# Reading transposed activations once from PSUM, a searched order of tasks at the edges, and adaLN units one place earlier, in a four-layer diffusion backbone

## The chip, the cores and the metric

The kernel runs on one core of a Trainium2 chip. Times are device microseconds (us) of that core from start to end of one execution. Lower is better. The kernel computes in fp32 accuracy: every large product is made of three fp32r products of high and low parts, so TensorE (PE) has three matmuls for each tile of a weight.

## What is computed

Four layers, each a token mixer (pooling, latent attention MLA, neighbourhood attention NA, pooling again) and a SwiGLU FFN, on 256 latent tokens and 256 context tokens of width 1024. Around each of the eight sub-layers stand two RMS norms, and shift, scale and gate come from a condition through one large matrix per layer (adaLN):

```python
def reference(x, c, ctx, c_ctx, ada_w, ada_b, norm_g, ...):
    for i in range(DEPTH):
        sh_m, sc_m, g_m, sh_f, sc_f, g_f = adaln(c[:, None, :], ada_w[i], ada_b[i])
        h_lat = modulate(rmsnorm(x, norm_g[i, 0]), sh_m, sc_m)      # h * (1 + scale) + shift
        ...                                                           # the same for ctx
        y_lat, y_ctx = mixer[i % 3](h_lat, h_ctx)
        x = x + g_m * rmsnorm(y_lat, norm_g[i, 1])
        f_lat = swiglu(modulate(rmsnorm(x, norm_g[i, 2]), sh_f, sc_f), ffn_w_gu[i], ffn_w_down[i])
        x = x + g_f * rmsnorm(f_lat, norm_g[i, 3])
        ...
    return x
```

The context stream ends after the mixer of layer 2 (counted from 0): from layer 2's FFN on only the latent tokens are worked on.

## The kernel before

**Tiling.** Tokens are four tiles of 128: tiles 0 and 1 are the latent stream (c = 0), 2 and 3 the context stream (c = 1). Activations that enter a product lie transposed, as eight blocks d of 128 features, each with a high and a low part (`R[d]`, `R[8 + d]`, tile `rh`). The hidden width of the FFN is 22 blocks of 128. While both streams run, a product has 512 columns; with one stream 256.

**Weights.** All weights and the adaLN matrices come in chunks of 512 KB through one DMA queue, issued by SP, into a ring of five tiles `raw`, in an order that a dry run of the program has recorded. ACT makes the high part of a chunk (L161, `wh`), DVE the low part (L165, `wl`), into five buffers each, up to five chunks ahead (`pump`). A slot of the ring is free when the last reader of its tile is issued, and the next load is issued then (`loads`).

**adaLN units.** A unit (l, u) is one sixth of a layer's adaLN matrix, in the order u = 1, 0, 2, 4, 3, 5, of eight steps with one `raw` tile each. A step is done either on PE from the raw tile (L406, `adp<-raw,sc`) or on DVE, which adds into `ff_a` (L424, L426), one instruction a step or, up to unit (2, 0), one for each stream; a unit with steps on DVE ends with pick products on PE (L406, `adp<-ff_a,pick`). Units that are not gates then go through an ACT copy (L451) and two PE transposes (L454). In an FFN each new weight chunk earns `RATE` steps (1.27, 1.27, 0.83, 0.5 by layer), done on DVE; `finish` ends a unit that has begun on DVE ahead of the last segment of the down projection; `need` does on PE, at once, what is missing when a result is wanted. The down projection has two segments of hidden blocks (12 and 10) with two streams and one of 22 with one stream; its products are L362 to L364 (`acc<-wh,rx`, `acc<-wl,rx`).

**Edges.** Between the last down (or output) products of one sub-layer and the first products of the next, the work on PE, DVE and ACT is ordered by a planner. `Edge` lists tasks (one or a few instructions) with an engine, a duration, dependences and a priority; `Sched.run` places them one after the other on modelled engines, by priority, and emits them by their modelled start. The tasks of an edge are: the last products of the projection (`second`); `chain`, for each token tile: squares (L864), output times gate (L870, L872), residual add (L881), squares for the next norm (L804), normalised x into `big` (L811 on DVE or L813 on ACT); `make_h`, for each pair of blocks d: transposes on PE into one PSUM bank (L916, `aux`), and from there the modulated high and low parts; and the first four chunks of the next sub-layer's products (`head`, L1087, L1088, L1090), with the weight splits they need. At the last pool mixer the products with the band and pool matrices (`mix_u`, `mix_y`, L1029) stand between a `make_h` and a second `chain` and `make_h`.

In `make_h` a transposed half bank of 256 columns (one d) is read from PSUM twice: once on ACT with scale, bias and rounding to fp32r (`high`, L930), and once on ACT (L935) or DVE (L937) into one of three tiles `t` (`whole`); DVE then subtracts the two (`low`, L940). Only at the first edge, where the shift arrives late, another form reads it once, into a tile `y` (`late_h`: L951 or L953, then L956 and L959).

Of the kernel before, what the change touches and what calls it, by code (L numbers as in the profile page):

```python
# [12 lines left out]
ALU = mybir.AluOpType  # L13
# [37 lines left out]

AHEAD = {'mwo': ('aux', 'aux'), 'nwo': ('aux', 'aux')}
# [21 lines left out]
class Net:  # L74
    def __init__(self, nc, pools, ins, out, uses=None, order=None):
# [17 lines left out]
        self.order = order  # L93
        self.rec = []
# [110 lines left out]
    def w(self, name, i, n=1):  # L205
# [411 lines left out]
class Slot:  # L617


    def __init__(self, before, old):  # L620
        self.before, self.old = before, old
        self.first, self.users, self.tile = None, [], None


class Sched:
# [9 lines left out]
    def add(self, eng, fn, deps=(), prio=5, order=(), ready=0.0, new=None, slots=(), between=False):  # L635
# [7 lines left out]
        t.new, t.between = new, between  # L643
        self.tasks.append(t)
        return t

    def slot(self, tag, bufs):
        a = self.tags.setdefault(tag, [])
        a.append(Slot(a[-1] if a else None, a[-bufs] if len(a) >= bufs else None))
        return a[-1]  # L650

    def run(self):
# [6 lines left out]
        busy = {e: [] for e in "PDAS"}  # L659
        left = list(enumerate(self.tasks))  # L660

        def place(e, at, dur, between):

            for a, b in busy[e]:
                if between:
                    at = b if a <= at < b - 0.1 else at
                    continue
                if at + dur - self.OVER[e] <= a:
                    break
                at = max(at, b)  # L670
            return at

        while left:
            can = [(t.prio, i, t) for i, t in left if all(d.end is not None for d in t.deps) and all(o.start is not None for o in t.order)]
            assert can, [(t.eng, t.prio) for _, t in left][:5]
            _, i, t = min(can, key=lambda x: x[:2])
            at = max([t.ready] + [o.start for o in t.order])
            options = []
            for e, dur in t.eng.items():
                s = place(e, max([at] + [d.end + (self.HOP if d.on != e else 0) for d in t.deps]), dur, t.between)  # L680
                options.append((s + dur, s, e))
            t.end, t.start, t.on = min(options)
            busy[t.on].append((t.start, t.end))
            busy[t.on].sort()
            left = [x for x in left if x[0] != i]

        for t in sorted(self.tasks, key=lambda t: (t.start, t.end)):
            self.emit(t)

# [9 lines left out]
class Edge:  # L699
# [6 lines left out]
    def __init__(self, n, l, u, tiles):  # L706
# [12 lines left out]
        self.spread = []  # L719

# [53 lines left out]
    def pooled(self, j):  # L774
        n = self.n
        return not n.dry and n.prepped + j - self.have < len(n.uses) and n.uses[n.prepped + j - self.have][0][1].startswith("pool")
# [54 lines left out]
    def chain_of(self, c, close):  # L831
# [3 lines left out]
        for t in (2 * c, 2 * c + 1):  # L835
            prio = 1 + t // 2 * 1.5
            gready = 0.0 if loads else 3.5
            done, sqs = {}, []
            for h in range(2):
                ps, made, slot, *ends = self.parts[t, h]  # L840
                y, hs = n.Y[2 * t + h], slice(512 * h, 512 * h + 512)
                p, gdeps = (1 + 0.4 * c, loads[c][h:h + 1]) if loads else (prio, [])
                if self.fold:
# [11 lines left out]
                    done[h] = s.add({"D": 0.56}, gy, [f, q] + gdeps, p, ready=gready)  # L855
# [3 lines left out]
                for e, (sl, g) in enumerate(gs):  # L859
# [5 lines left out]
                    sqs.append(s.add({"A": 0.68 if g is None else 0.5}, sq, made, p, slots=(slot,)))  # L865
# [7 lines left out]
                    ys.append(s.add({"D": 0.69 if g is None else 0.42}, gy, made + gdeps, p, slots=(slot,), ready=gready))  # L873
                done[h] = ys[-1]
# [3 lines left out]
            for h in range(2):  # L878
# [5 lines left out]
                new[h] = s.add({"D": 0.7}, up, [fac, done[h]], prio)  # L884
# [3 lines left out]
    def make_h(self, l, i):  # L888
# [8 lines left out]
        for c in self.streams:  # L897
# [5 lines left out]
            for dp in range(4):  # L903
                tag = "acc" if late and i == 0 and c == 0 else "aux"
# [14 lines left out]
                for e in range(2):  # L919
# [4 lines left out]
                    if late:  # L924
# [1034 lines left out]
```

## Time and profile before

| what | value |
|---|---|
| time, median of 3 runs | 1735.46 us (1735.09 to 1737.63) |
| the profiled execution: its time | 1739.13 us |
| the profiled execution: span of its trace | 1737.4 us |
| PE busy | 1635.4 us, 94% of the span |
| DVE, ACT busy | 1065.8 us (61%), 754.7 us (43%) |
| granted TensorE clock, mean | 0.97 of full speed |
| bytes moved by DMA | 286.66 MB, mean 165 GB/s |

In the trace an instruction is named by its line, its engine and output<-inputs; `[1.46 <-DMA raw]` behind a line is idle time of the engine ahead of it, and what ended it. PE is busy nearly everywhere; time can be lost or won where it is not, and where its clock is below full speed.

### The profile page before, as it was taken

How to read it: one execution, taken by the hardware profiler on the slowest of the kernel's cores; microseconds unless marked ns; L12 is line 12 of the kernel's file. 1: busy time of each engine (PE TensorE's matmuls, PEld its weight loads, DVE VectorE, ACT ScalarE, POOL GpSimd, SP SyncE). 2: the span in 40 equal slices, each digit the busy share in tenths (PEclk: the TensorE clock that was granted, in tenths of full speed). 3: DMA queues.
4: the chain of work that ended last, by engine and by line, in shares of the span. 5: the costliest groups of instructions: out<-in, count | busy, mean ns of one | idle time of the engine just before them, and what ended most of it. 6: DMA issues, size and time to landing. Idle time of an engine off the chain costs nothing.

```text
span 1737.4 us, 24716 instructions
## 1 busy us (share of the span) xinstructions
PE 1635.4 (94%) x9686; PEld 1378.5 (79%) x9686; DVE 1065.8 (61%) x1715; ACT 754.7 (43%) x1348; POOL 34.1 (2%) x42
## 2 busy tenths in 40 slices
PE   5899999999989999899999999999979999769998
PEld 2588888888886777888888888888769997659996
DVE  3567766664657674677545536765657773567554
ACT  4663223222554445522232226654565543464442
POOL 0000000000000110000000000000000000000000
PEclk8999999999999999999999999999989999879999
DMA  8926566554221131365654541433338896228662
GB/s 327 338 68 222 191 194 188 165 171 162 73 85 43 55 122 61 110 205 184 199 193 159 195 157 65 137 113 118 101 127 287 285 303 208 108 95 311 195 186 93
DMA packets 82525, 286.66 MB, mean 165 GB/s; under 512 B 9788, under 2 KB 12648, under 8 KB 82408
## 3 DMA queue, kind: packets, MB, share of 16 engines
q1 hardware_dynamic: 79208, 278.71, 48.2%
q0 software_dynamic: 1760, 5.29, 1.0%
q8 instruction: 76, 1.25, 0.3%
q10 hardware_dynamic: 1440, 1.09, 0.2%
q14 instruction: 41, 0.34, 0.1%
HBM read 283.95 MB, written 1.09 MB: 164 GB/s over the span
## 4 chain that ended last, share of the span: by engine, by line
PE 86%; DVE 6%; ACT 6%; DMA 1%; issue 1%; DVEq 0%; SPq 0%; ACTq 0%
PE acc L354 14%; PE acc L355 14%; PE acc L356 13%; PE acc L362 8%; PE acc L363 8%; PE acc L364 8%; PE adp L406 3%; PE acc L1088 2%; PE acc L1087 2%; PE acc L1090 2%; PE aux L354 1%; PE aux L355 1%; PE aux L356 1%; PE aux L916 1%; DVE wl L165 1%
## 5 line engine op out<-in xcount | busy, mean ns | idle before, releaser
L165 DVE TENSOR_TENSOR wl<-raw,wh 128x1024 fp32r<-128x1024 f32 x321 | 389.1, 1222 | 218.2 <-ACT wh L161 216.7
L161 ACT ACTIVATE wh<-raw 128x1024 fp32r<-128x1024 f32 x321 | 334.3, 1053 | 334.9 <-PE acc L364 159.0
L354 PE MATMUL acc<-rh,wh 128*128 128x512 f32 (+1 forms) x1296 | 439.0, 339 | 0.0
L355 PE MATMUL acc<-rh,wh 128*128 128x512 f32 (+1 forms) x1296 | 436.6, 337 | 0.0
L356 PE MATMUL acc<-rh,wl 128*128 128x512 f32 (+1 forms) x1296 | 436.5, 337 | 0.0
L354 PEld LDWEIGHTS acc<-rh,wh 128*128 128x128 f32 x1296 | 246.0, 190 | 30.5 <-issue 4.1
L356 PEld LDWEIGHTS acc<-rh,wl 128*128 128x128 f32 x1296 | 246.0, 190 | 25.8
L355 PEld LDWEIGHTS acc<-rh,wh 128*128 128x128 f32 x1296 | 246.1, 190 | 25.0
L426 DVE SCALAR_TENSOR_TENSOR ff_a<-raw,sc,ff_a 128x1024 f32<-128x1024 f32 x168 | 209.5, 1280 | 0.2
L362 PE MATMUL acc<-wh,rx 128*128 128x512 f32 x528 | 207.0, 392 | 0.0
L363 PE MATMUL acc<-wl,rx 128*128 128x512 f32 x528 | 205.9, 390 | 0.0
L364 PE MATMUL acc<-wh,rx 128*128 128x512 f32 x528 | 205.7, 390 | 0.0
L391 ACT ACTIVATE rx<-big 128x256 fp32r<-128x256 f32 (+1 forms) x82 | 42.4, 517 | 251.9 <-DVE big L556 251.9
L556 DVE TENSOR_TENSOR big<-big,acc 128x256 f32<-128x256 f32 (+1 forms) x90 | 48.9, 543 | 116.8 <-PE acc L356 96.1
L364 PEld LDWEIGHTS acc<-wh,rx 128*128 128x128 f32 x528 | 99.4, 188 | 20.8
L362 PEld LDWEIGHTS acc<-wh,rx 128*128 128x128 f32 x528 | 99.4, 188 | 20.2
L363 PEld LDWEIGHTS acc<-wl,rx 128*128 128x128 f32 x528 | 99.4, 188 | 20.2
L1087 PE MATMUL acc<-rh,wh 128*128 128x256 f32 x304 | 82.8, 299 | 6.4 <-ACT wh L161 3.2
L1088 PE MATMUL acc<-rh,wl 128*128 128x256 f32 x304 | 81.7, 296 | 6.2 <-DVE wl L165 5.9
L916 PE MATMUL aux<-ident,big 128*128 128x128 f32 x192 | 37.3, 329 | 46.1 <-DVE big L811 27.0
L377 DVE TENSOR_TENSOR rx<-big,rx 128x256 fp32r<-128x256 f32 (+1 forms) x82 | 45.0, 549 | 47.8 <-ACT rx L391 47.8
L916 PEld LDWEIGHTS aux<-ident,big 128*128 128x128 f32 x192 | 25.7, 166 | 58.2 <-DVE big L811 28.7
(239 smaller groups left out, 2267.4 us busy)
## 6 DMA issues: line engine op xcount, KB each, us to landing
raw<-in_ada_w SPq DMA_DIRECT2D x192, 512.0 KB, 4.8
raw<-in_gu SPq DMA_DIRECT2D x176, 512.0 KB, 4.6
raw<-in_dn SPq DMA_DIRECT2D x88, 512.0 KB, 4.3
raw<-in_nwin SPq DMA_DIRECT2D x24, 512.0 KB, 3.7
G<-gate POOLq DMA_DIRECT2D x10, 512.0 KB, 4.8
raw<-in_mwo SPq DMA_DIRECT2D x8, 512.0 KB, 3.5
raw<-in_nwo SPq DMA_DIRECT2D x8, 512.0 KB, 3.9
raw<-in_mwin SPq DMA_DIRECT2D x6, 512.0 KB, 3.4
```

The source lines that it names most:

```text
L161: nc.scalar.activation(out=hi[:, 0:n, :], in_=raw, func=AF.Copy)
L165: nc.vector.tensor_tensor(out=lo[:, 0:n, :], in0=raw, in1=hi[:, 0:n, :].bitcast(F32), op=ALU.subtract)
L354: nc.tensor.matmul(out, wh, ah, start=start, stop=False)
L355: nc.tensor.matmul(out, wh, al, start=False, stop=False)
L356: nc.tensor.matmul(out, wl, ah, start=False, stop=stop)
L362: nc.tensor.matmul(out, ah, wh, start=start, stop=False)
L363: nc.tensor.matmul(out, ah, wl, start=False, stop=False)
L364: nc.tensor.matmul(out, al, wh, start=False, stop=stop)
L426: nc.vector.scalar_tensor_tensor(out=acc[:, i, :], in0=v, scalar=c, in1=acc[:, i, :], op0=ALU.mult, op1=ALU.add)
L916: nc.tensor.transpose(slot.tile[:, o:o + 128], xs.tile[:, j:j + 128], n.ident)
L1087: nc.tensor.matmul(o, wh, hi, start=(k == 0), stop=False)
L1088: nc.tensor.matmul(o, wl, hi, start=False, stop=False)
```

## The change

Three things are changed.

1. `make_h` uses one form at every edge (`split_h`): x times the norm factor is read once from PSUM, by ACT or DVE, with scale and shift, into a tile Y in SBUF; `high` is made from it on ACT or DVE, `low` on DVE. The tiles `t` are gone. With one stream the third pair of banks is taken from `adp`.
2. The planner tries 1500 random changes of the priorities (with a fixed seed) and keeps those that its model finds better; the model has a new rule, that ACT and DVE do not work on the same PSUM bank at once. Some durations, priorities and dependences in the list are changed: squares come before the gate product of the same bank, weight splits of pool chunks are counted, and so on. Plans are found in the dry run and used again.
3. In layer 1's FFN the units from (2, 2) on get 1.7 steps for each chunk in place of 1.27. With one stream the down projection gives 6 of its 22 steps of the second half to the edge, where it gave 10, and closes an open unit ahead of the edge.

```diff
+SEARCH = 1500
+RATE_ONE = 1.7
...
@@ def w
-            self.credit += self.rate
+            l, u = self.ada_now[0] if self.ada_now else (self.ada_todo or [(0, 0)])[0]
+            self.credit += RATE_ONE if self.rate == RATE[1] and (l, u) >= (2, 2) else self.rate
...
@@ class Sched, def run (place is the old placing, with the loop over a bank's readers new)
+        if best is None:
+            rng = random.Random(1)
+            best = [t.prio for t in self.tasks]
+            cost = self.place(best)
+            for r in range(search):
+                width, share = rng.choice((0.05, 0.3, 1.5)), rng.choice((0.01, 0.05, 0.3))
+                some = [p + rng.uniform(-width, width) if rng.random() < share else p for p in best]
+                c = self.place(some)
+                if c <= cost:
+                    best, cost = some, c
+        self.place(best)
...
+                while e != "P":
+                    hit = [b for x in t.banks for a, b, f in banks[x] if a < s + dur and s < b and f != e]
+                    if not hit:
+                        break
+                    s = free(e, max(hit), dur, t.between)
...
+        return busy["P"][-1][1] + 0.02 * sum(t.end for t in tasks) / len(tasks)
...
@@ class Edge, def chain
-                    sqs.append(s.add({"A": 0.68 if g is None else 0.5}, sq, made, p, slots=(slot,)))
+                    q = s.add({"A": 0.82 if g is None else 0.66}, sq, made, p, slots=(slot,))
+                    sqs.append(q)
...
-                    ys.append(s.add({"D": 0.69 if g is None else 0.42}, gy, made + gdeps, p, slots=(slot,), ready=gready))
+                    ys.append(s.add({"D": 0.69 if g is None else 0.42}, gy, [q] + made + gdeps + free, p + 0.02, slots=(slot,), ready=gready))
...
@@ def make_h
-                tag = "acc" if late and i == 0 and c == 0 else "aux"
+                tag = "acc" if late and i == 0 and c == 0 else "adp" if len(self.streams) == 1 and dp == 2 else "aux"
...
-                    def high(ps=ps, hi=hi, a=a, b=b):
-                        nc.scalar.activation(out=hi, in_=ps(), func=AF.Identity, scale=a, bias=b)
...
-                            nc.scalar.activation(out=tmp.tile, in_=ps(), func=AF.Identity, scale=a, bias=b)
...
-                        nc.vector.tensor_tensor(out=lo, in0=tmp.tile, in1=hi.bitcast(F32), op=ALU.subtract)
+                    self.hs[c, d] = self.split_h(ps, n.Y[4 * c + dp][:, 256 * e:256 * e + 256], a, b, hi, lo, trs, ua, ub, slot, prio)
+                    self.in_y[4 * c + dp] = self.in_y.get(4 * c + dp, []) + self.hs[c, d]
...
@@ def split_h (was late_h; late: the first edge)
+                    nc.scalar.activation(out=y, in_=ps(), func=AF.Identity, scale=a, bias=b)
...
+                nc.vector.tensor_scalar(out=y, in0=ps(), scalar1=a, scalar2=b, op0=ALU.mult, op1=ALU.add)
...
+                nc.vector.tensor_scalar(out=hi, in0=y, scalar1=b if late else 1.0, scalar2=None, op0=ALU.add if late else ALU.mult)
...
+                nc.scalar.activation(out=hi, in_=y, func=AF.Copy)
...
+                nc.vector.tensor_tensor(out=lo, in0=y, in1=hi.bitcast(F32), op=ALU.subtract)
+        w = s.add({"D": 0.53, "A": 0.56}, part, trs + ua, prio - 0.06, slots=(slot,))
+        q = s.add({"A": 0.48, "D": 0.32}, high, [w] + ub, prio)
         return [s.add({"D": 0.42}, low, [w, q], prio), q]
...
@@ the FFN's down projection
-        k0 = max(0, nk - 2 * W_BUFS)
+        k0 = 0 if two else nk - 2 * (W_BUFS - 2)
         begun = [n.acc() for _ in tiles] if k0 else None
         for k in range(k0):
             for t in tiles:
                 product(begun[t], t, 1, k)
+        if not two:
+            n.finish(True)
```

How it moves instructions is shown at three places. In these lists L numbers are those of the kernel that is listed, and behind them stand the operation, its output and inputs, and how often it comes in a row.

PE in layer 2's down projection, before: the products with `rx` are those of the FFN's hidden blocks, `adp` belongs to an adaLN unit (3.3).

```order
L364 MATMUL acc<-wh,rx_27_153 128x512
L406 MATMUL adp<-raw,sc 32x256 x32
L454 MATMUL adp<-ident,ada 128x128 x2
L362 MATMUL acc<-wh,rx_28_154 128x512
L363 MATMUL acc<-wl,rx_28_154 128x512
```

After, that place has down products alone. PE in layer 1, ahead of the last segment of its down projection, after (unit 3.0; L364 to L366 are products of the last gate and up chunk, L416 was L406, L464 was L454, L372 was L362):

```order
L364 MATMUL acc<-rh,wh 128x512
L365 MATMUL acc<-rh,wh 128x512
L366 MATMUL acc<-rh,wl 128x512
L416 MATMUL adp<-raw,sc 32x256 x24
L416 MATMUL adp<-ff_a,pick 32x256 x4
L464 MATMUL adp<-ident,ada 128x128 x2
L372 MATMUL acc<-wh,rx_16_142 128x512
```

Eight steps on PE have left layer 2; six steps with pick products and transposes now stand in layer 1, where before there was no unit at that place.

DVE at the edge from NA to its FFN (one stream), `make_h`, before:

```order
L811 TENSOR_SCALAR big<-xt,st 128x512
L937 TENSOR_SCALAR t<-aux,mod_137,m_134 128x256 x2
L940 TENSOR_TENSOR rh<-t,rh 128x256 x3
L937 TENSOR_SCALAR t<-aux,mod_137,m_134 128x256
L940 TENSOR_TENSOR rh<-t,rh 128x256 x2
L937 TENSOR_SCALAR t<-aux,mod_137,m_134 128x256
L940 TENSOR_TENSOR rh<-t,rh 128x256 x3
L165 TENSOR_TENSOR wl<-raw,wh 128x1024 x6
```

and after (L869 was L811, L174 was L165):

```order
L869 TENSOR_SCALAR big<-xt,st 128x512
L174 TENSOR_TENSOR wl<-raw,wh 128x1024
L1005 TENSOR_SCALAR rh<-y_103 128x256
L1015 TENSOR_TENSOR rh<-y_103,rh 128x256
L1005 TENSOR_SCALAR rh<-y_103 128x256
L1005 TENSOR_SCALAR rh<-y_105 128x256
L1015 TENSOR_TENSOR rh<-y_105,rh 128x256
```

DVE no longer reads PSUM there (the eight reads are on ACT), makes six of the eight `high` (L1005) and all `low` (L1015), and one weight split stands ahead of them.

ACT at the second `make_h` of the edge from layer 2's FFN through the last pool mixer, before:

```order
L813 ACTIVATE big<-xt,st 128x512
L935 ACTIVATE t<-aux,m_132,mod_135 128x256
L930 ACTIVATE rh<-aux,m_132,mod_135 128x256 x3
L935 ACTIVATE t<-aux,m_132,mod_135 128x256
L930 ACTIVATE rh<-aux,m_132,mod_135 128x256 x2
L935 ACTIVATE t<-aux,m_132,mod_135 128x256
L930 ACTIVATE rh<-aux,m_132,mod_135 128x256 x2
L935 ACTIVATE t<-aux,m_132,mod_135 128x256
L930 ACTIVATE rh<-aux,m_132,mod_135 128x256
L161 ACTIVATE wh<-raw 128x1024 x6
```

and after (L871 was L813, L170 was L161):

```order
L871 ACTIVATE big<-xt,st 128x512 x2
L997 ACTIVATE y_103<-aux,m_132,mod_135 128x256
L997 ACTIVATE y_104<-aux,m_132,mod_135 128x256 x2
L997 ACTIVATE y_105<-adp,m_132,mod_135 128x256
L1009 ACTIVATE rh<-y_105 128x256
L997 ACTIVATE y_105<-adp,m_132,mod_135 128x256
L997 ACTIVATE y_106<-aux,m_132,mod_135 128x256 x2
L1009 ACTIVATE rh<-y_106 128x256
L170 ACTIVATE wh<-raw 128x1024 x2
```

Twelve reads of PSUM by ACT have become seven; two weight splits follow where six did.

## Rows read from the trace of the kernel before

**Rows 1.** The page: busy us, share of the span and instructions of each engine.

```profile
PE 1635.4 (94%) x9686; PEld 1378.5 (79%) x9686; DVE 1065.8 (61%) x1715; ACT 754.7 (43%) x1348; POOL 34.1 (2%) x42
```

**Rows 2.** Stretches: start:end, width, busy us of PE, PEld, DVE, ACT, POOL; clock; DMA.

```profile
83.00:110.00 27.00, 20.68 (x154) 19.66 (x154) 16.88 (x43) 18.22 (x49) 0.00 (x0) 0.94 0.23 77
464.00:490.00 26.00, 22.39 (x153) 20.52 (x153) 20.70 (x48) 21.57 (x45) 0.00 (x0) 0.94 0.24 83
685.00:712.00 27.00, 20.27 (x130) 17.87 (x129) 19.40 (x45) 20.46 (x44) 0.00 (x0) 0.94 0.23 78
740.00:760.00 20.00, 20.00 (x89) 16.54 (x89) 17.72 (x17) 5.03 (x7) 0.00 (x0) 1.00 0.73 238
1064.00:1090.00 26.00, 23.10 (x163) 20.77 (x162) 20.36 (x46) 21.03 (x43) 0.00 (x0) 1.00 0.26 82
1270.00:1296.00 26.00, 15.19 (x67) 12.23 (x66) 16.18 (x38) 16.46 (x34) 0.00 (x0) 0.74 0.16 57
1320.00:1340.00 20.00, 20.00 (x169) 20.00 (x168) 17.45 (x22) 9.68 (x15) 0.00 (x0) 1.00 0.94 325
1496.00:1545.00 49.00, 23.72 (x132) 20.38 (x131) 32.70 (x76) 35.11 (x79) 0.00 (x0) 0.69 0.11 36
```

**Rows 3.** PE's instructions in order, 1470 to 1482: start, length, what, idle before.

```profile
1470.01 1.93 PE L406 MATMUL adp<-raw,sc 128*32 128x256 f32 x32
1476.83 1.08 PE L406 MATMUL adp<-raw,sc 128*32 128x256 f32 x8 [2.79 <-DMA raw<-in_ada_w]
1480.99 0.69 PE L454 MATMUL adp<-ident,ada 128*128 128x128 f32 x2 [0.51 <-ACT ada L451]
1481.33 0.78 PE L362 MATMUL acc<-wh,rx 128*128 128x512 f32 x1
1481.90 0.63 PE L363 MATMUL acc<-wl,rx 128*128 128x512 f32 x1
```

**Rows 4.** The page, DMA issues: KB each, us to landing.

```profile
raw<-in_ada_w SPq DMA_DIRECT2D x192, 512.0 KB, 4.8
```

**Rows 5.** Chain of waits, 1270 to 1296: start, length, what.

```profile
1283.30 0.70 PE aux L916 x2
1284.02 0.57 ACT t L935
1284.62 0.55 DVE t L937
1285.20 1.03 ACT rh L930 x2
...
1291.37 1.23 DVE wl L165
1292.64 0.58 PE acc L1088
```

**Rows 6.** Groups of instructions over the whole run: busy us, mean ns, idle before.

```profile
L930 ACT ACTIVATE rh<-aux,m,mod 128x256 fp32r<-128x256 f32 x72 | 38.7, 564 | 9.5 <-DVE t L937 9.2
L940 DVE TENSOR_TENSOR rh<-t,rh 128x256 fp32r<-128x256 f32 x72 | 30.5, 424 | 11.1 <-ACT rh L930 10.3
L956 ACT ACTIVATE rh<-y,m 128x256 fp32r<-128x256 f32 x32 | 14.8, 502 | 1.7 <-DVE m L458 0.8 <-DVE y L953 0.6
L811 DVE TENSOR_SCALAR big<-xt,st 128x512 f32<-128x512 f32 x27 | 13.1, 487 | 0.9
```

**Rows 7.** Chain of waits, 1496 to 1545.

```profile
1504.49 0.70 PE aux L916 x2
...
1516.80 0.88 PE acc L1029 x5
...
1531.34 0.70 PE aux L916 x2
...
1539.04 0.95 ACT wh L161
...
1541.30 0.58 PE acc L1088
```

More of the change, by code (lines that the diff above doesn't have):

```diff
@@ L643, in add @@
         t.new, t.between = new, between
+        t.banks = [s for s in (new, *slots) if s and s.tag in ("acc", "aux", "adp")]
         self.tasks.append(t)
@@ L665, in place, with free @@
+        for t in sorted(self.tasks, key=lambda t: (t.start, t.end)):
+            self.emit(t)
+        return best
+    def place(self, prios):
+        busy = {e: [] for e in "PDAS"}
+        banks = collections.defaultdict(list)
+        tasks = self.tasks
+        def free(e, at, dur, between):
+            b = busy[e]
+            k = max(bisect.bisect_left(b, (at,)) - 1, 0)
+            for i in range(k, len(b)):
+                x, y = b[i]
                 if between:
-                    at = b if a <= at < b - 0.1 else at
+                    at = y if x <= at < y - 0.1 else at
@@ L667, in place @@
                     continue
-                if at + dur - self.OVER[e] <= a:
+                if at + dur - self.OVER[e] <= x:
                     break
-                at = max(at, b)
+                at = max(at, y)
             return at
[L673 to L677, printed above, removed]
+        left = [len(set(d + o)) for d, o in self.links]
@@ L681, in run @@
                 options.append((s + dur, s, e))
             t.end, t.start, t.on = min(options)
[L683 to L688, printed above, removed]
+            bisect.insort(busy[t.on], (t.start, t.end))
+            if t.on != "P":
+                for x in t.banks:
+                    banks[x].append((t.start, t.end + self.HOP, t.on))
@@ L690, in emit @@
+            for j in self.after[i]:
+                left[j] -= 1
+                if not left[j]:
+                    heapq.heappush(can, (prios[j], j))
+        assert n == len(tasks)
+        return busy["P"][-1][1] + 0.02 * sum(t.end for t in tasks) / len(tasks)
     def emit(self, t):
@@ L1017, in mix_y @@
         tiles = (2 * c, 2 * c + 1)
-        for t, h in [(t, h) for h in range(2) for t in tiles] if tag == "acc" else [(t, h) for t in tiles for h in range(2)]:
+        for t, h in [(t, h) for h in range(2) for t in tiles] if self.end_units and c == 0 else [(t, h) for t in tiles for h in range(2)]:
             slot = self.slot(tag)
@@ L1054, in spread_gate @@
             m = s.add({"P": 0.9}, spread, [self.end_units[2]], prio, new=slot)
-            self.gate[c].append(s.add({"A": 0.58}, copy, [m], prio, slots=(slot,)))
+            self.gate[c].append(s.add({"A": 0.58}, copy, [m] + used, prio, slots=(slot,)))
     def banded(self):
```

95 lines of the change are left out of this document (56 added, 39 removed).

## The prediction

> **What bounds the kernel now.** I read the busy line of the page first, then a table of busy time by stretches, then the chain of waits inside the two stretches with one stream. TensorE is busy for 1635.4 us of a span of 1737.4 us [rows 1]. By the order of instructions the matmuls are the same before and after (9307 against 9303 on PE), so only two things can move the time: the roughly 100 us in which TensorE is idle, and the stretches in which its granted clock is low because it was idle just before. [rows 2] show where that is. I call the stretches between two big products edges: E1 (464 to 490, pool FFN to MLA), E2 (685 to 712, MLA to its FFN), E3 (1064 to 1090, FFN to NA), E4 (1270 to 1296, NA to its FFN), E5 (1496 to 1545, FFN through the last pool mixer to the last FFN). The idle time of PE is the width less the PE column: 3.6, 6.7, 2.9, 10.8 and 25.3 us, and the clock column is 0.74 and 0.69 in the last two, 0.94 or more in the others. The first edge with work on all engines (83 to 110) has 6.3 us. One further hole is not a planned edge at all: the burst at 1470 [rows 3]. Nothing else is worth much.
>
> **The change, part by part.** The sum is made against the profiled execution's own time, 1739.1 us (1.7 us beyond its span); the median of the runs shown is 3.7 us below it.
>
> *A, adaLN unit 3.3 leaves layer 2's down projection: +12.4 us.* Its eight steps run on PE in one go in the middle of the down products. The first four find their tiles loaded (x32, 1.93 us; the trace counts each matmul of a step twice); the others wait for DMA, one of them 2.79 us, and the products that stopped at 1470.0 come back at 1481.3: 11.3 us [rows 3]. The products behind it start 0.43 to 0.57 us apart (1481.33, 1481.90) where 89 records in 20 us say 0.225 us [rows 2], for about five of them: 1.1 us more. The order of after has nothing of a unit in that place, and the unit's steps lie on DVE in the FFN, where PE has 20.00 of 20 us [rows 2]. Bounds 11 to 12.4. The gate units 3.2 and 3.5 move forward by one place with their POOL transfers; POOL is busy for 34.1 us in all [rows 1], so that costs nothing.
>
> *B, a new burst in layer 1: −8 us.* Moving a unit ahead by one means that unit 3.0 is open when layer 1's FFN ends: two of its steps have run on DVE, and six (24 matmuls) are now emitted on PE ahead of the last down segment, with the pick products and two transposes behind. No such place is in the trace; the nearest is [rows 3]. Five steps at 1.93/4 us are 2.4 us if five tiles wait in the ring of five; the sixth can be asked for only when the first step has freed a slot, and then 4.8 us pass to landing [rows 4]: 0.5 + 4.8 = 5.3 us, or 6.8 us if it takes the 6.3 us that the tile used at 1476.83 took from the slot freed by the first step at 1470.5. Then come the step (0.5), the pick products (0.4), the wait for ACT's copy (0.51) and the transposes (0.34): 7.0 to 8.6 us. If all six lie there it is 3.4 us; if it goes as at 1470 and costs clock too, 10.5. I take 8. Queued behind it on SP are six down chunks; five prepared chunks of 24 products (24 × 0.225 = 5.4 us each) cover them.
>
> *C, pick products directly ahead of their transposes in two places of layer 1: −1.0 us*, since PE then waits for ACT's copy, 0.51 us each [rows 3]; 0 to −1.5.
>
> *D, E4: +3.7 us.* [rows 5] show one transposed bank (two halves of 256 columns): transposes of 0.70 us end at 1284.0, then the bank is read by ACT, by DVE and by ACT twice more, one after the other, until 1286.2; only then can PE write the next transposes. The other banks follow, the weight split L165 is in DVE's queue behind them, and the head has its operands at 1292.64. After, one read per half: eight halves on ACT. The nearest row for such a read is L930, 564 ns [rows 6]: 4.5 us. The last `low` (424 ns) stands behind, and the order shows a weight split moved ahead of DVE's part. From 1283.30: 0.7 + 4.5 + 0.4 = 5.6, so 1288.9 instead of 1292.6. What becomes late next is DVE: six `high`, eight `low`. A `high` on DVE from SBUF to SBUF is not in the trace. From above it is bounded by L811 (487 ns at twice the width) and L940 is near (424 ns, same width, two operands); from below I take half of L811, 0.24. I take 0.42, so 14 × 0.42 = 5.9 us, of which the part ahead of ACT's last read is hidden. That the tile t0 now ends only 18 products (4.1 us) ahead of t1, where it was 30, can take back up to 2.7 us. Bounds 0 to 6.5, the low clock of this edge included.
>
> [...]
>
> *E, E5: +9 us.* Two norm chains, two `make_h` and the pool mixer between them [rows 7]. The transposes at 1504.49 and 1531.34 each open an eight-half stretch like E4's. The second ends with the weights: ACT makes `wh` of a head chunk only at 1539.04, `wl` follows on DVE, and the head runs in full from 1541.30. In the order of after, two splits stand behind `make_h` on ACT where six did, so the head waits for its operands alone: transposes, seven reads on ACT (DVE takes one), a `high` and a `low`, 0.7 + 7 × 0.56 + 0.4 + 0.4 = 5.4 us instead of 10.0: +4.6. The first `make_h` feeds the mixer's products, 12.3 us from its transposes to those of 1516.80; its reads are a part of that and no weights wait there: I take a third of the 4.6, +1.4. The norm chains ahead of both `make_h` (1496 to 1504.49, and 1516.80 to 1531.34 with four mixer outputs in it, 23 us together) are only put in another order, with the two tiles' steps side by side: I take an eighth, +3. Bounds 0 to 14.
>
> *F, the two-stream edges:* idle 3.6, 6.7, 2.9 us [rows 2] is the most that each can give. The reads per bank halve in each; I take two thirds: +2.5, +4.5, +2. Bounds 0 to 13. *G, the start:* +1.5 of 6.3 idle us [rows 2] by the new task order, bounds −3 to +5; up to 83 us the order of loads sets it, and that stays.
>
> Sum: 12.4 − 8 − 1 + 3.7 + 9 + 9 + 1.5 = 26.6. 1739.1 − 26.6 = 1712.5; less 3.7 is **1709 us**.
>
> **Rivals.** *1, the edges keep their length.* The chain at an edge is norm statistics, then reads, then weights; if ACT and DVE are the bound and not the bank, their work hardly falls (per half three operations of 0.5 us as before). Then D to G give a third of 23.2, 8 us, and with A, B and C 11.4 us: 1727.7 − 3.7 = 1724. For it: ACT and DVE are busy for 35.1 and 32.7 of 49 us in E5 [rows 2]; against it: that is two thirds, so waits for each other, not work, make the length.
> *2, the edges give nearly all.* D to G at about nine tenths of the way to their bounds (6, 12, 11, 3) and B at 6: 12.4 − 6 − 1 + 32 = 37.4, so 1698.
> *3, the burst only changes its place.* B costs 12.4 as A did: 22.2 us in all, 1713; it lies within my own range, and is part of the forecast's chance.
> *4, slower: loads bound layer 1.* At 1.7 steps per chunk 2.7 tiles pass the ring of five in the 5.4 us of a chunk; a tile may then be held for 5 × 5.4/2.7 = 10 us. If asking, landing and waiting for DVE take 12 us, a chunk takes 6.5 us, 1.1 us more for about 25 chunks (42 steps at 1.7): 27 us, which is all of the sum; above 12 us a tile the kernel is slower, at 12.5 us by 6 us (1742). For it: landing alone takes 4.8 us [rows 4]. Against it: in 1320 to 1340 the kernel before moved 325 GB/s with PE busy for 20.00 of 20 us [rows 2]; that is 6.5 MB or 12 tiles, so five slots turned over in 8 us. On DVE a step of these units is one instruction, where in 740 to 760, with DVE at 17.72 of 20 us and PE at 20.00 [rows 2], a step was two (both streams).
> *5, it does not do what it says:* if the plan that the search found under its model is no better on the chip than the old one, and the new SBUF reads are longer, D to G give −4 and A to C 3.4: 1736, within 0.2% of before.
>
> **How the numbers follow.** Forecast with rival 3: 0.52, 1703 to 1717. Rival 1: 0.22. Rival 2: 0.15. Rival 4: 0.04 and the worse side of rival 5, 0.02, are slower; the rest of rival 5, 0.05, is the same. The range leaves out rivals 4 and 5 and the far half of rival 2: 1696 to 1727. About 0.2% (3.5 us) is what a measurement of this kernel can tell from no change; rivals 1 to 3 and the forecast are all faster than that: 0.89, 0.05, 0.06.
>
> **What would show it.** A: no adp product with a DMA wait at layer 2's down projection. B: a hole of 7 to 9 us between 1010 and 1035 us (some 54 us of down products ahead of E3's end) with adp products in it. D, E: PE idle in E4 near 7 us and in E5 near 16, and per half one read of the bank. F: no wait above 1 us on a reader of aux in the three edges. G: the mixer of layer 0 ends within 2 us of before. Rival 4 would show as PE below 20.00 in a 20 us window of layer 1's FFN. I am wrong if the edges' idle time stays above three quarters, or if DVE, which takes most `high` and all `low`, ends the waits of the single-stream edges.

## The result, and the profile after

The changed kernel takes 1690.1 us (1687.6 to 1691.3) where the kernel before took 1736.6 us; the ratio is 0.9728, 95% interval 0.9709 to 0.9747. The direction was forecast, the size was not: 46 us were gained, 27 forecast, and the time lies 6 us below the range (1696 to 1727).

The busy line of the page of after, to be held against [rows 1]; columns are busy us, share of the span, instructions:

```profile
span 1688.2 us, 24684 instructions
PE 1624.0 (96%) x9678; PEld 1374.2 (81%) x9678; DVE 1068.2 (63%) x1756; ACT 728.8 (43%) x1309; POOL 34.1 (2%) x42
```

The span is 49.2 us shorter. PE is busy for 11.4 us less, although it has the same products of the layers (8 records of adaLN products are gone), and idle for 37.8 us less (102.0 and 64.2 us, span less busy time). So about a quarter of the gain is not idle time at all. The next table says where most of it comes from. Stretches of after, at the same places of the program as [rows 2] (they begin 6 to 36 us earlier now): start:end, width, busy us of PE, PEld, DVE, ACT, POOL, granted clock, DMA share, GB/s:

```profile
458.00:482.00 24.00, 23.84 (x176) 22.41 (x175) 20.04 (x50) 18.36 (x39) 0.00 (x0) 1.00 0.27 89
665.00:690.00 25.00, 25.00 (x148) 22.00 (x147) 20.21 (x55) 18.51 (x46) 0.00 (x0) 1.00 0.22 72
1053.00:1079.00 26.00, 26.00 (x182) 24.14 (x182) 20.91 (x55) 19.26 (x44) 0.00 (x0) 1.00 0.25 82
1255.00:1277.00 22.00, 17.76 (x82) 14.83 (x81) 18.31 (x43) 16.55 (x37) 0.00 (x0) 0.84 0.44 144
1460.00:1500.00 40.00, 27.19 (x173) 23.96 (x172) 33.66 (x88) 31.30 (x76) 0.53 (x1) 0.87 0.20 66
```

E1, E2 and E3 are closed: PE is busy for 23.84 of 24, 25.00 of 25 and 26.00 of 26 us, where 3.6, 6.7 and 2.9 us were idle, and the clock is 1.00 where it was 0.94 in E1 and E2. In E4 and E5 4.2 and 12.8 us are idle (10.8 and 25.3 before), and the clock is 0.84 and 0.87 (0.74 and 0.69). The clock records of these two traces have two levels, 1.00 and 0.50 of full speed, and in these stretches the lower stands where PE had been idle. With a mean granted clock of 0.974 before and 0.985 after, 2 × 0.026 × 1737 = 90 us and 2 × 0.015 × 1688 = 51 us were at the lower level. PE was busy in 55.1 and 40.4 us of that, by the clock records of the two traces. Products of 512 columns start 0.43 us apart at the lower level in B of after (1007.15 and 1007.58) and 0.23 us apart at the upper (from 1010.40 on), so these 14.7 us fewer account for an estimated 14.7 × (1 − 0.23/0.43) = 6.8 of the 11.4 us; the rest I have not traced. The head's products show what the lower level costs. The chain of waits of after, in E5 (start, length, what):

```profile
1490.41 0.50 DVE big L869
1490.95 1.12 PE aux L976 x4
...
1495.15 0.12 PE acc L1145
1495.27 0.12 PE acc L1146
```

Those products of 256 columns lie 0.12 us apart, with the clock at 1.00 (1495 to 1496). In E5 of before, right behind 1541.30 [rows 7], the same products lay 0.21 us apart, with the clock at 0.50 (1541.8 to 1543.0):

```profile
1541.88 0.21 PE acc L1087
1542.10 0.21 PE acc L1088
```

From the transposes at 1490.95 to the head are 4.2 us; before, from 1531.34 to 1541.30, 10.0.

To see where the time went, I took PE's matmuls without those of the adaLN units, in order (8950 in each trace), and compared the start of the n-th in both. The stretches are cut at fixed n: E1 from 2000 to 2120, E2 3000 to 3360, E3 4780 to 5100, E4 6100 to 6300, E5 7490 to 7700, and the places of A (7300 to 7490) and B (4400 to 4640).

| stretch | before, us | after, us | gain | forecast |
|---|---|---|---|---|
| start, to the 440th | 121.6 | 116.4 | 5.2 | 1.5 |
| E1 | 18.6 | 14.6 | 4.0 | 2.5 |
| E2 | 66.8 | 57.4 | 9.4 | 4.5 |
| layer 1's FFN, with the first wait of C | 241.8 | 243.0 | −1.2 | −1.0 |
| B, with the second wait of C | 55.2 | 64.9 | −9.7 | −8 |
| E3 | 48.9 | 45.1 | 3.8 | 2 |
| E4 | 45.8 | 38.7 | 7.1 | 3.7 |
| A | 55.6 | 43.1 | 12.5 | 12.4 |
| E5 | 61.6 | 45.7 | 15.9 | 9 |

The first row is uncertain: kernels with the same order of products there as after needed 112.2 to 117.4 us for it in the runs below. At the edges, kernels with the same order of instructions agree within 0.2 us at E1 and E2, 1.1 us at E3 and E4 and 2.1 us at E5 (45.7 in after, 47.8 in e5, where 10.2 and 20.5 us were at the lower clock). The adaLN terms A, B and C came out near what was worked; the five edges gave 40.2 us where D, E and F said 21.7. By the same cut about 31 us of these are idle time of PE and 9 are shorter busy time.

B is seen in PE's instructions in order (start, length, what, idle before):

```profile
989.00 0.44 PE L464 MATMUL adp<-ident,ada 128*128 128x128 f32 x2 [1.22 <-ACT ada L461]
...
1000.28 2.37 PE L416 MATMUL adp<-raw,sc 128*32 128x256 f32 x40
1004.84 0.64 PE L416 MATMUL adp<-raw,sc 128*32 128x256 f32 x8 [2.19 <-DMA raw<-in_ada_w]
1005.30 0.61 PE L416 MATMUL adp<-ff_a,pick 128*32 128x256 f32 x8
1006.48 0.44 PE L464 MATMUL adp<-ident,ada 128*128 128x128 f32 x2 [0.56 <-ACT ada L461]
1006.67 0.68 PE L372 MATMUL acc<-wh,rx 128*128 128x512 f32 x1
```

Five steps were loaded (40 records), the sixth waited for its DMA, and the transposes waited 0.56 us for ACT's copy: 6.4 us. The first row is another unit's transposes (C), which waited 1.22 us; most of the remaining 2 us of this stretch are products at the low clock behind the burst (e1, with the same burst at full clock, loses 8.1 us here and not 9.7).

### The profile page after: what moved, and what is told of

The parts are those of the page before. It is cut to its first block, busy times and chain, and to the rows that moved or that the text cites. A ratio compares the mean times of both kernels' runs of the same rounds, so it can differ in the third digit from the quotient of the medians.

```text
span 1688.2 us, 24684 instructions
## 1 busy us (share of the span) xinstructions
PE 1624.0 (96%) x9678; PEld 1374.2 (81%) x9678; DVE 1068.2 (63%) x1756; ACT 728.8 (43%) x1309; POOL 34.1 (2%) x42
## 5 line engine op out<-in xcount | busy, mean ns | idle before, releaser
L174 DVE TENSOR_TENSOR wl<-raw,wh 128x1024 fp32r<-128x1024 f32 x321 | 389.3, 1221 | 209.1 <-ACT wh L170 206.6
L170 ACT ACTIVATE wh<-raw 128x1024 fp32r<-128x1024 f32 x321 | 335.0, 1052 | 330.3 <-PE acc L374 157.3
L364 PE MATMUL acc<-rh,wh 128*128 128x512 f32 (+1 forms) x1296 | 438.6, 338 | 0.0
L366 PE MATMUL acc<-rh,wl 128*128 128x512 f32 (+1 forms) x1296 | 436.5, 337 | 0.0
L364 PEld LDWEIGHTS acc<-rh,wh 128*128 128x128 f32 x1296 | 246.0, 190 | 29.2 <-issue 2.9
L366 PEld LDWEIGHTS acc<-rh,wl 128*128 128x128 f32 x1296 | 246.0, 190 | 26.0
L372 PE MATMUL acc<-wh,rx 128*128 128x512 f32 x528 | 207.1, 392 | 0.0
L566 DVE TENSOR_TENSOR big<-big,acc 128x256 f32<-128x256 f32 (+1 forms) x90 | 48.9, 543 | 117.4 <-PE acc L366 98.0
L372 PEld LDWEIGHTS acc<-wh,rx 128*128 128x128 f32 x528 | 99.5, 188 | 21.3 <-issue 0.8
L1146 PE MATMUL acc<-rh,wl 128*128 128x256 f32 x304 | 78.2, 286 | 0.0
L387 DVE TENSOR_TENSOR rx<-big,rx 128x256 fp32r<-128x256 f32 (+1 forms) x82 | 45.0, 549 | 47.8 <-ACT rx L401 47.8
L1427 ACT ACTIVATE big<-big,mx 128x512 f32<-128x512 f32 (+1 forms) x64 | 42.5, 665 | 60.0 <-DVE big L1582 31.7
L416 PE MATMUL adp<-raw,sc 128*32 128x256 f32 x496 | 42.6, 431 | 18.7 <-ACT big L862 9.3
```

The source lines that it names most:

```text
L170: nc.scalar.activation(out=hi[:, 0:n, :], in_=raw, func=AF.Copy)
L174: nc.vector.tensor_tensor(out=lo[:, 0:n, :], in0=raw, in1=hi[:, 0:n, :].bitcast(F32), op=ALU.subtract)
L364: nc.tensor.matmul(out, wh, ah, start=start, stop=False)
L366: nc.tensor.matmul(out, wl, ah, start=False, stop=stop)
L372: nc.tensor.matmul(out, ah, wh, start=start, stop=False)
L566: nc.vector.tensor_tensor(out=b, in0=b, in1=psu[:, sl], op=ALU.mult)
```

## The experiments

Two theories of the missing 20 us stood first. Theory 1: the second read of each PSUM bank kept PE waiting, and the single read gave most. Theory 2: the plan gave most. All times are medians, each with the interval of its ratio to the kernel before on the same chip; the runs lie on several chips, so what a part loses is a difference of medians that can be 1 to 2 us off. "Edges" is the sum of E1 to E5 by the cut above, in one trace of each kernel (241.7 us before, 201.5 after).

**e1: the units' places alone**, in the kernel before.

```diff
-            self.credit += self.rate
+            l, u = self.ada_now[0] if self.ada_now else (self.ada_todo or [(0, 0)])[0]
+            self.credit += RATE_ONE if self.rate == RATE[1] and (l, u) >= (2, 2) else self.rate
...
+        if not two:
+            n.finish(True)
         edge = Edge(n, l, 5, tiles)
```

> The kernel before with nothing changed but the places of the adaLN units (1.7 steps a chunk for the one-stream units in layer 1's FFN, and an open unit closed ahead of the single-stream edge). By the trace of after against before, matched by the same matmul, unit 3.3's leaving gives 12.6 us, the burst of unit 3.0 in layer 1 costs 8.2 and the two waits for ACT's copy 1.2 to 1.7. Both theories of the edges expect 1736.6 - 12.6 + 8.2 + 1.5 = 1733.7 us (1732 to 1736). If the units' places also shorten the edges, below 1728.

Measured 1736.7 us, ratio 0.9995 (0.9983 to 1.0006): no change, a little above the 1732 to 1736 expected. The trace has A at 12.5 us of gain, B at 8.1 of loss and C at 1.2 of loss; E3 and E5 are 1.1 and 1.5 us longer, which eats the rest. So the new places of the units, by themselves, are worth nothing: the gain of after lies in the edges.

**e2: the single read alone**, with the old planner.

```diff
-                    tmp = self.slot("t")
-                    ... (high, whole and low from PSUM and t)
+                    self.hs[c, d] = self.split_h(ps, n.Y[4 * c + dp][:, 256 * e:256 * e + 256], a, b, hi, lo, trs, ua, ub, slot, prio)
```

> The kernel before with one thing changed: at every edge the transposed half bank is read once from PSUM into Y, high and low are made from there; planner, durations, priorities and units as before. Theory 1 (the second read of each bank kept PE waiting, and the single read gave most of the 47 us that the edges gained): 30 us or more of the 47, so 1700 to 1710 us. Theory 2 (the searched plan gave most; with the old plan the single read is one more step in a chain): 1728 to 1738 us.

Measured 1729.0 us, 0.9956 (0.9939 to 0.9972). Theory 1 is wrong: 7 us, not 30. Edges 235.5 us; E4 gains 0.5 us and E5 1.1. What PE waits for in E5 of this kernel (total us, times, longest):

```profile
PE aux L916 <- DVE big L811: 16.5, 4, 7.5
PE acc L1082 <- ACT wh L161: 3.2, 1, 3.2
PE aux L916 <- ACT y L936: 1.9, 3, 0.8
```

The reads' own wait has fallen (1.9 us; it was 4.0 us in this place in the kernel before), but the norm chain and the weights, in the same order as before, end as late as before.

**e3: two reads**, in the changed kernel.

```diff
-                    self.hs[c, d] = self.split_h(...)
+                    if late:
+                        self.hs[c, d] = self.split_h(...)
+                        continue
+                    tmp = self.slot("t")
+                    ... (high, whole and low as before the change)
```

> The changed kernel with the old make_h: each half bank read twice from PSUM (high on ACT, whole on ACT or DVE), searched plan, new rule on banks and units' places kept. Theory 1: it loses 30 us or more, 1718 to 1728 us. Theory 2: it keeps most of the gain, 1693 to 1703 us.

Measured 1699.3 us, 0.9779 (0.9763 to 0.9796): 9 us are lost. Edges 211.3: the loss is in E3 (49.1, +4.0) and E5 (51.8, +6.1), with 1.0 in E2. E1 and E4 lose nothing (14.5 and 37.5). The longest waits of PE at E3 are not on a bank:

```profile
PE acc L1790 <- ACT rx L401: 1.4, 1, 1.4
PE acc L1165 <- DVE wl L174: 0.9, 1, 0.9
```

**e4: no search.**

```diff
-SEARCH = 1500
+SEARCH = 0
```

> The changed kernel with no tries (the first plan, by the priorities as written, is taken). Theory 1: little lost, 1691 to 1700 us. Theory 2: the search is where the edges' 47 us come from, 1712 to 1737 us. Between, 1700 to 1712, the two would share.

Measured 1703.8 us, 0.9811 (0.9795 to 0.9827): 13.7 us are lost, between the two theories. Edges 216.5, most of it in E2 (65.3, +7.9) and E5 (49.2, +3.5). PE's waits at E2 in this kernel:

```profile
PE acc L1145 <- DVE y L930: 3.3, 1, 3.3
PE aux L976 <- DVE big L869: 1.4, 1, 1.4
```

The first is the wait that E2 had in the kernel before, where the head's products need a bank that a gate product (L870 there) still has to read:

```profile
PE acc L1087 <- DVE y L870: 3.1, 1, 3.1
```

With the search it is gone: PE waits for nothing in E2 of after (25.00 of 25 us). Without the search 25 us of the edges' 40 remain, and the single read alone gave 6 (e2), so a third cause was to be found.

**e5: no burst in layer 1.** At 1.9 steps a chunk unit 3.0 ends on DVE.

```diff
-RATE_ONE = 1.7
+RATE_ONE = 1.9
```

> The changed kernel with 1.9 steps a chunk in place of 1.7 for the one-stream units: unit 3.0 then ends on DVE inside layer 1's FFN and the six steps on PE ahead of the last down segment are gone. If the burst costs what the matched traces say (8.2 us there), 1682 us (1680 to 1685). Rival: at 2.9 tiles a chunk the loads or DVE hold the products up in layer 1's FFN (PE under 20.00 in a 20 us window), and the time is 1690 us or more.

Measured 1682.8 us (1681.2 to 1685.3), 0.9676 (0.9656 to 0.9696). That is faster than both kernels, by 7.4 us than the changed one. B's stretch falls from 64.9 to 57.7 us. The start is 4.2 us shorter in this trace and E5 2.1 us longer, both within what the same code varies by. The rival, loads as the bound, does not show in the time; a stretch of this run:

```profile
840.00:860.00 20.00, 20.00 (x90) 16.57 (x89) 11.83 (x11) 6.54 (x8) 0.00 (x0) 1.00 0.84 279
```

PE is busy for 20.00 of 20 us with 279 GB/s. Of eight stretches between 740 and 980 us one is under it (880 to 900, 19.50), and there PE waits 0.5 us for ACT's copy, as in after, and not for loads.

**e6 and e7: the share of down steps left to the single-stream edge**, 10 in the changed kernel (e6), 6 in the kernel before (e7).

```diff
-        k0 = 0 if two else nk - 2 * (W_BUFS - 2)
+        k0 = max(0, nk - 2 * W_BUFS)
```

> The changed kernel with the old share of the single-stream down projection in the edge (10 of 22 steps of the second half, not 6). Theory a (fewer steps leave two weight buffers free, so that the head's and the pool's weights are ready; that is where E4 and E5 gained): 1697 to 1704 us, lost at E4 and E5 alone. Theory b (the order and the bank rule gave it): 1688 to 1693 us.

> The kernel before with that one change of the share (6 steps, not 10). Theory a: E4 and E5 gain 5 us or more together, 1724 to 1731 us. Theory b: 1733 to 1739 us.

Measured: e6 1694.9 us, 0.9741 (0.9719 to 0.9763); e7 1731.0 us, 0.9960 (0.9945 to 0.9975). e7 lies at the upper end of theory a's range; e6 lies between the two ranges, and its ratio is not clear of that of the changed kernel. What decides is the place: E5 is 53.6 us in e6 (+7.9) and 56.3 in e7 (−5.3), and E4, which follows an output projection and not a down projection, does not move (37.9 and 45.8). So theory a holds for E5 alone. In e7 the head's waits for weights that E5 had in the kernel before (3.2 us on `wh`, 0.7 on `wl`) are gone. In e6 PE waits for weights too, but at the pool mixer's products; its head, in the new order, does not:

```profile
PE acc L372 <- ACT wh L170: 2.3, 1, 2.3
PE acc L373 <- DVE wl L174: 0.7, 1, 0.7
```

**e8: no rule on banks** in the model.

```diff
-                while e != "P":
-                    hit = [b for x in t.banks for a, b, f in banks[x] if a < s + dur and s < b and f != e]
-                    if not hit:
-                        break
-                    s = free(e, max(hit), dur, t.between)
```

> The changed kernel with a planner that again lets ACT and DVE work on one PSUM bank at once in its model (the chip still takes them in turn). If the rule is what makes the searched plan hold on the chip: 1695 to 1705 us, with waits for aux readers at E1 to E3. If not: 1688 to 1693 us.

Measured 1697.1 us, 0.9755 (0.9736 to 0.9774): 7 us lost by the medians, spread over E2, E3 and E5 (+1.5, +2.3, +2.2); the ratio overlaps that of the changed kernel at its edge, and E5's part is no more than the same order varies by. The waits on readers of aux that were expected at E1 to E3 show at E3 alone (1.3 us). That ACT and DVE take one bank in turn is seen in [rows 5]: each of the two changes of engine there comes 0.03 us after the other's read has ended.

**e9: two banks** for the transposes of the single-stream edges.

```diff
-                tag = "acc" if late and i == 0 and c == 0 else "adp" if len(self.streams) == 1 and dp == 2 else "aux"
+                tag = "acc" if late and i == 0 and c == 0 else "aux"
```

> The changed kernel with the transposes of the single-stream edges in the two aux banks alone (the change gives the third pair of blocks the adp bank). Theory c: the third bank is why E4 keeps its 7 us of gain in every run so far but those with the old list of tasks, and part of E5's 16: 1695 to 1702 us, lost at E4 and E5. Against it: 1688 to 1693 us.

Measured 1695.0 us, 0.9749 (0.9728 to 0.9769): 4.9 us lost by the medians, with ratios that overlap; E5 +4.3, E4 +0.5. Theory c is wrong for E4; for E5 the trace speaks for it.

**e10: the old squares**, and **e11, e12: two tries to better e5.**

```diff
-                    q = s.add({"A": 0.82 if g is None else 0.66}, sq, made, p, slots=(slot,))
+                    q = s.add({"A": 0.68 if g is None else 0.5}, sq, made, p, slots=(slot,))
...
-  ... gy, [q] + made + gdeps + free, p + 0.02, ...
+  ... gy, made + gdeps + free, p, ...
```

```diff
 e11, e12: RATE_ONE = 1.9
-        k0 = 0 if two else nk - 2 * (W_BUFS - 2)
+        k0 = 0 if two else nk - 2 * (W_BUFS - 3)     (e11)
-SEARCH = 1500
+SEARCH = 6000                                        (e12)
```

> The changed kernel with squares and gate products of a bank in no given order and with the old durations of squares (0.68 and 0.5 in place of 0.82 and 0.66). Theory d: that order is what lets the norm chains of E4 and E5 end earlier: 1694 to 1702 us. Against it: 1688 to 1693 us.

> The kernel without layer 1's burst (1.9 steps a chunk) and with 4 of 22 down steps left to the single-stream edges in place of 6, so that a third weight buffer is free. If free buffers go on shortening E5: 1678 to 1681 us. If the second tile's chain, which then starts only 12 products after the first's, is late instead: 1684 to 1690 us.

> The kernel without layer 1's burst and with 6000 tries in place of 1500. If the model still finds what holds on the chip: 1677 to 1681 us. If the plans are at the end of what the model knows: 1681 to 1685 us.

Measured: e10 1687.4 us, 0.9710 (0.9693 to 0.9727), edges 202.4: nothing lost, theory d is wrong as long as the bank rule stands. e11 1687.7 us, 0.9709 (0.9693 to 0.9725), and e12 1684.4 us, 0.9689 (0.9672 to 0.9707): neither is faster than e5, and their edges are those of e5 within 0.5 us each. e11's 5 us lie outside the edges, 3.4 of them in the start and MLA, where runs of the same code differ by as much; that a third free buffer costs anything is not shown.

**e13 and e14: a model that knows nothing of the banks.** By then E4's 7 us had survived every single change; only kernels with the old planner's list lacked them. DVE's weight splits against its norm outputs show what those kernels share. In E4 before (DVE in order of time):

```profile
1266.45 2.36 DVE L165 TENSOR_TENSOR wl<-raw,wh 128x1024 fp32r<-128x1024 f32 x2 [2.01 <-ACT wh L161]
1277.25 0.49 DVE L811 TENSOR_SCALAR big<-xt,st 128x512 f32<-128x512 f32 x1
1282.75 0.49 DVE L811 TENSOR_SCALAR big<-xt,st 128x512 f32<-128x512 f32 x1
1291.37 5.76 DVE L165 TENSOR_TENSOR wl<-raw,wh 128x1024 fp32r<-128x1024 f32 x5
```

and in E4 after:

```profile
1254.40 3.69 DVE L174 TENSOR_TENSOR wl<-raw,wh 128x1024 fp32r<-128x1024 f32 x3 [2.01 <-ACT wh L170]
1263.42 2.35 DVE L174 TENSOR_TENSOR wl<-raw,wh 128x1024 fp32r<-128x1024 f32 x2
1268.76 0.88 DVE L869 TENSOR_SCALAR big<-xt,st 128x512 f32<-128x512 f32 x2
1270.27 0.49 DVE L869 TENSOR_SCALAR big<-xt,st 128x512 f32<-128x512 f32 x1
```

Before, two splits are done ahead of the norm outputs and the others wait behind `make_h`; after, five stand ahead. The head takes two chunks and then needs the third. PE's waits show it, in E4 before

```profile
PE aux L916 <- DVE big L811: 5.0, 2, 4.8
PE acc L1088 <- DVE wl L165: 3.7, 1, 3.7
```

and in E4 after, where the wait for `wl` is gone:

```profile
PE aux L976 <- DVE big L869: 4.0, 2, 3.8
```

In e4, without search, three splits stand ahead, and that sufficed. The edit of e13 and e14 is that of e8 and e10 together; e13 has SEARCH = 0 as well.

> The changed kernel with a model that knows nothing of the banks (no rule, squares and gate products in no given order and with their old durations) and without tries. If the third weight split's place is what E4 gained: E4 is back near 45.8 us (from 39.1 without the search alone) with PE waiting for wl there, and the time is 1708 to 1716 us. If the single read or the third bank gave E4's gain: E4 stays near 39 and the time is 1700 to 1706 us.

> The same blind model with the search of 1500 tries. If the search alone suffices for the third split: E4 39 us, and the time 1695 to 1700 us (as with the bank rule alone taken away). If the search needs the model's knowledge of the banks to be of use on the chip: 1701 to 1712 us.

Measured: e13 1720.2 us, 0.9894 (0.9879 to 0.9909), somewhat above the range of its theory; edges 228.2, E4 45.0. Its DVE and its PE at E4:

```profile
1268.70 2.36 DVE L174 TENSOR_TENSOR wl<-raw,wh 128x1024 fp32r<-128x1024 f32 x2 [2.01 <-ACT wh L170]
...
1292.49 5.76 DVE L174 TENSOR_TENSOR wl<-raw,wh 128x1024 fp32r<-128x1024 f32 x5
```

```profile
PE acc L1141 <- DVE wl L174: 5.0, 1, 5.0
PE aux L971 <- DVE big L864: 3.2, 2, 3.1
```

With the single read, the third bank and the new share all in place, E4 has its old length, and PE waits 5.0 us for the third split. The same holds in all sixteen traces. The five kernels with two splits ahead of the norm outputs (before, e1, e2, e7, e13) have PE waiting 3.7 to 5.0 us for `wl` and an E4 of 45.0 to 45.8 us; the eleven with three or more have no such wait and 37.5 to 39.2 us. No run moved that split alone.

e14 took 1702.1 us (1696.3 to 1705.3), 0.9779 (0.9752 to 0.9806). The time lies in the second range, but E4 is back at 39.0, as the first theory said; edges 211.7. So the search alone finds the third split's place; with a blind model it still leaves 10 us in the edges, of which 3.0 lie in E2, 2.3 in E3 and 4.0 in E5.

Against after, the edges lose 15.0 us without the search (e4), 10.2 without the model's knowledge (e14) and 26.7 without both (e13). In the sum the two nearly add up (25.2 and 26.7), but not place by place: at E4 each alone is enough (39.1 and 39.0 us), and only without both is E4 long. So taking away single parts (e3, e4, e6, e8, e9) did not show E4's cause.

## Why the prediction was right and wrong

**A and B: right, C too small.** 12.5 us against 12.4 for A; −10.9 against −9.0 for B and C together. The burst moved as worked: five tiles loaded, the sixth late by its landing. What I had only as the upper bound, the low clock behind it, came as well. e5, without the burst, gains 7.4 us, and its stretch of B is 7.2 us shorter (−8 forecast); that leaves 3.7 us for the two places of C, where I had 1.0; the second wait alone is 1.22 us and not 0.51. A slip: "if all six lie there" is 4.1 us by its own terms (6 × 0.48 + 0.4 + 0.51 + 0.34), not 3.4.

**F, the edges with two streams: the step that failed** is "idle 3.6, 6.7, 2.9 us is the most that each can give", and the two thirds taken of it. They gave 4.0, 9.4 and 3.8, more than the most: 17.2 us against 9. Nearly all of the idle time went (by the cut 2.6, 6.7 and 2.9 us), and with it 5.0 us of busy time. In E1 and E2 PE had been busy at the low clock for 2.7 and 3.3 us behind the holes, and is for none now; at the spacings of 0.43 and 0.23 us that is an estimated 2.8 of the 5.0 us. [rows 2] had it in the clock column (0.94 in E1 and E2), and I read that column without pricing it. In E3 the clock was 1.00 before as well, and why its busy time fell by 0.9 us stays open. Over the whole kernel shorter busy time is 11.4 us; my sum had 1.1 us of it, in A, and left it at bounds in D.

The mechanism of F, the reads per bank, is not what closed these edges either. With two reads put back (e3) E1 loses nothing and E2 1.0 us; E2 hangs on the plan, and loses 7.9 us without the search (e4). E3 loses 4.0 us in e3, but PE waits there for `rx` and `wl` (1.4 and 0.9 us) and not for a reader of aux. At all edges together the single read alone gave 6 of the 40 us (e2). D, E and F each came out above the upper bound that I had given (7.1, 15.9 and 17.2 us over 6.5, 14 and 13).

**D, E4: the mechanism was wrong.** 7.1 us against 3.7, and none of it is the single read: e3 has two reads and an E4 of 37.5 us, e2 has one and 45.3, and e13 has one read, 45.0 us and the wait for `wl`. I had the row (1291.37, `wl` behind the other banks) and the order with a split moved ahead, and gave the 3.7 us to the reads. Going by what ended last, the wait of the head for `wl`, would have pointed to the split.

**E, E5: several parts, sized too low.** 15.9 us against 9. The last 4.6 us, from transposes to the head, were 5.8 (10.0 to 4.2). The share of down steps, which I had not priced, is worth 5 to 8 us of E5 (e7, e6): under the old order it ends the head's wait for weights, which I had put to the order of splits, and under the new order a wait at the pool mixer's products. The single read gave about 6 (e3), the third bank, which I had not priced either, about 4 (e9), the search 3.5 (e4). Of each of these losses 2.0 to 3.4 us are idle time of PE; what e3, e6 and e9 lose beyond that is longer busy time, with more of it at the low clock, which differs by 2 us between kernels with the same order. The norm chain, of which I took an eighth, gave more: of the waits of before in E5

```profile
PE aux L916 <- DVE big L811: 16.8, 4, 7.5
PE aux L916 <- ACT rh L930: 4.0, 3, 1.9
PE acc L1087 <- ACT wh L161: 3.2, 1, 3.2
```

the first fell by 5.8 us, though it still holds the longest wait of after there:

```profile
PE aux L976 <- DVE big L869: 11.0, 2, 7.2
```

**A price taken too high.** A `high` on DVE, which I set to 0.42 us between 0.24 and 0.49, and the one on ACT:

```profile
L1005 DVE TENSOR_SCALAR rh<-y 128x256 fp32r<-128x256 f32 x46 | 13.0, 292 | 2.6 <-ACT y L997 1.9
L1009 ACT ACTIVATE rh<-y 128x256 fp32r<-128x256 f32 x26 | 10.6, 416 | 2.1 <-DVE y L1001 1.5
```

On DVE it took 0.292 us. Two groups on ACT have like operands, one per partition, from SBUF (L1007) and from PSUM (L995):

```profile
L1007 ACT ACTIVATE rh<-y,m 128x256 fp32r<-128x256 f32 x21 | 9.1, 499 | 1.2 <-DVE m L468 0.8 <-DVE y L999 0.3
L995 ACT ACTIVATE y<-aux,mod 128x256 f32<-128x256 f32 x15 | 6.3, 466 | 4.7 <-PE aux L976 4.7
```

The one from SBUF takes 33 ns more. But the new `high` on ACT has no per-partition operand and takes 416 ns, less than the read from PSUM that it replaced (564 ns, [rows 6]), so the longer reads from SBUF of rival 5 did not come with the change.

**G** went the right way, and its size stays open: the start took 118.5 to 121.6 us in three traces with the old order and 112.2 to 117.4 in six with the new one. The 1.5 us are less than either spread, and "within 2 us of before" does not hold for the two profiled executions (5.2 us).

**The signs.** PE waits in E1 to E3 of after for no reader of aux, as forecast. The burst came at 1000 to 1007 us and not at 1010 to 1035, since the edges ahead of it gave more. PE is idle for 4.2 and 12.8 us in E4 and E5, where I had 7 and 16. DVE does end the waits that are left there, 4.0 and 11.0 us, which I had named as a sign of being wrong; but it ends them with the norm outputs `big`, not with `high` or `low`.

**The rivals.** Rival 2 (1698) was the nearest, and had 0.15; its edges stayed under the same bounds, as did the low end of the range. Rival 1, at 0.22, had the argument that ACT's and DVE's work hardly falls. That is so (DVE 1065.8 and 1068.2 us, ACT 754.7 and 728.8), and yet the edges closed: waits for each other made the length, as the counter-argument said. Rival 3 did not come: the burst cost 7.2 us and not 12.4. Rival 4 did not happen, not even at 1.9 steps a chunk (e5).

## What to carry to other kernels

Price a hole on the matmul engine by its idle time and by the granted clock behind it: here a quarter of the gain was shorter busy time, an estimated six tenths of that from fewer products at the low clock. Idle time alone is no upper bound. Where a plan sets the order, look first for the wait that ends last, and which small task of another engine would end it: with a third weight split ahead of the norm outputs E4 was 6 us shorter, and either the search alone or the model's rule and order without a search put it there. Parts that replace each other so must be taken away together, since taking away one shows no loss.

## What the runs showed of the hardware

The low clock was met only behind idle time of PE in the stretches shown, but the same hole did not always bring it. In B of after, behind the wait of 2.19 us, the granted clock is at its lower level (0.50 of full speed from 1007 to 1010), and the products take 0.63 us; from 1010.40 on they take 0.39 again:

```profile
1009.28 0.63 PE L372 MATMUL acc<-wh,rx 128*128 128x512 f32 x1
1010.40 0.39 PE L372 MATMUL acc<-wh,rx 128*128 128x512 f32 x1
```

In e1 the same burst has a wait of 2.27 us, and the clock stays at full speed (1.00 from 1022 to 1026), with products of 0.39 us:

```profile
1020.25 0.64 PE L409 MATMUL adp<-raw,sc 128*32 128x256 f32 x8 [2.27 <-DMA raw<-in_ada_w]
1022.86 0.39 PE L365 MATMUL acc<-wh,rx 128*128 128x512 f32 x1
```

At E3 it is the other way round: behind a hole of 2.07 us the clock is 1.00 in the kernel before (1087 to 1093) and 0.72 in e1 (1094 to 1100), with the same order of instructions. So what the clock adds to a hole differs here between executions by 1 to 2 us (1.6 us in B, where 9.7 and 8.1 us were lost, and 1.1 us at E3).

The start of a run varies too: the first 440 matmuls of kernels with the same order there ended between 112.2 and 117.4 us (after, e3, e5, e6, e9, e11), and between 118.5 and 121.6 us with the old one (before, e1, e7).
